# A 3x3 convolution on one core: the first load in two transfers, and rows of one-word loads between the stores

## The chip, the core and the metric

The kernel runs on one core of one Trainium2 chip. The metric is the device time of one execution in microseconds, as the median of several runs. A profile of one execution, taken by the hardware profiler, goes with it; its times count from the span's start, and its own span is a little different from the measured time.

## The reference

Sixteen images of 64 channels and 64 x 64 pixels are convolved with 128 filters of 3 x 3, padding 1, all in float32. Nine tenths of the weights are zero, at random places; the kernel makes no use of that.

```python
x_pad = np.pad(x, ((0, 0), (0, 0), (pad, pad), (pad, pad)), mode='constant')
output = np.zeros((batch, c_out, h, w), dtype=np.float32)
...
                        if weight[co, ci, kh, kw] != 0:
                            output[b, co] += weight[co, ci, kh, kw] * x_pad[b, ci, kh:kh+h, kw:kw+w]
```

The input is 16.8 MB, the output 33.6 MB.

## The kernel before

The 16 images are taken as eight pairs. A pair's 2 x 64 channels lie on the 128 partitions (`xs[p]`, bfloat16), so that one image uses the upper half of TensorE's rows and the other the lower half. Each pair is computed in four blocks of 16 rows.

Loads. All of the input but 32 rows is loaded by GpSimd's DMA queue, which casts float32 to bfloat16 on the way: the lower half of pair 0, pairs 1 to 3 and a part of pair 4 at once (L63 to L77), the rest one pair at a time behind the additions of pairs 1 to 5 (L196 to L199). The weights (`w_sb`, L60) and the first 32 rows of pair 0 (`x_head`, L62, `HEAD = 32`) go through SyncE's queue (SP) in float32. `x_head` is a buffer of the output pool and is cast in three pieces by `cast_x`: rows 0 to 9 by VectorE (L123), rows 9 to 18 and 18 to 32 by ScalarE (L130 and L133). The first eight output rows need only the first piece, the next eight the second too.

Computing. The weights are cast, transposed by TensorE and combined into five groups. Block 0 of pair 0 is computed directly (`direct`, L159). All others go through `twos` (L166): GpSimd adds neighbouring rows into `s`, TensorE makes one shared product from it (copied out of PSUM by ScalarE as `pc`) and one for the even and one for the odd rows, and VectorE adds `pc` to those (L183) into the output tile `o`. Until the input is there, TensorE runs matmuls on zeros (`keep_busy`, L84).

Stores. When the four blocks of a pair are done, SP stores both images, 2 MB each (L209). The last pair is stored in halves of 1 MB (L206): two behind block 1, two behind block 3. Output tiles come from a pool of seven buffers, `x_head` among them, so a tile's first write waits for the store of the tile seven before it.

The order on SP is the order of the code: an instruction that waits holds up all behind it. Every transfer that SP issues takes the next of eight completion semaphores in turn. Where a semaphore is taken again, the program has a wait on it first, until its former transfer has landed. So the wait of each transfer on SP is for the one eight before it (and, for a store, for VectorE's last addition). Behind the stores of pair 1 there are four loads of one word each into `spare`, which nothing reads (L216).

A transfer over 128 partitions has 128 packets of data, eight on each of the core's 16 DMA engines, and one event per engine when it has landed.

Of the kernel before, what the change touches and what calls it, by code (L numbers as in the profile page):

```python
# [8 lines left out]
FP32 = mybir.dt.float32  # L9
# [18 lines left out]
def kernel(  # L28
# [6 lines left out]
    nc = tc.nc  # L35
# [2 lines left out]
    C_OUT, _, KH, KW = weight.shape  # L38
    assert (B, C_IN, H, W) == (16, 64, 64, 64) and (C_OUT, KH, KW) == (128, 3, 3)
    NP = B // 2  # L40
    HEAD = 32

    const_pool = ctx.enter_context(tc.tile_pool(name="const", bufs=1))
    x_pool = ctx.enter_context(tc.tile_pool(name="x", bufs=1))
# [10 lines left out]
    def pair(p):  # L55
        return x[2 * p : 2 * p + 2].rearrange("n i h w -> (n i) h w")
# [2 lines left out]
    w_sb = const_pool.tile([C_OUT, C_IN * KH * KW], FP32, name="w_sb")  # L59
    nc.sync.dma_start(out=w_sb, in_=weight.rearrange("o i kh kw -> o (i kh kw)"))  # L60
    x_head = o_pool.tile([128, H, W], FP32, name="o")
    nc.sync.dma_start(out=x_head[:, 0:HEAD, :], in_=pair(0)[:, 0:HEAD, :])  # L62
    nc.gpsimd.dma_start(out=xs[0][:, HEAD:H, :], in_=pair(0)[:, HEAD:H, :])  # L63
    ident = const_pool.tile([128, 128], BF16, name="ident")
    make_identity(nc, ident)

    def load(p, a=0, b=H):
        nc.gpsimd.dma_start(out=xs[p][:, a:b, :], in_=pair(p)[:, a:b, :])  # L68
# [15 lines left out]
    def keep_busy(n):  # L84
        for _ in range(n):
            nc.tensor.matmul(idle_ps, idle_rhs[:, 0:128], idle_rhs, start=True, stop=True)  # L86
# [13 lines left out]
    def cast_x(copy, a, b):  # L100
        copy(out=xs[0][:, a:b, :], in_=x_head[:, a:b, :])  # L101
# [12 lines left out]
    def difference(g, wps):  # L114
        nc.vector.tensor_tensor(out=wT[:, g], in0=wps, in1=wT[:, G1], op=SUB)  # L115
# [11 lines left out]
    ps2 = transposed(G2)  # L127
    nc.scalar.copy(out=wT[:, G2], in_=ps2)
    keep_busy(7)
    cast_x(nc.scalar.copy, 9, 18)  # L130
    difference(G01, ps0)
    difference(G21, ps2)
    cast_x(nc.scalar.copy, 18, HEAD)  # L133


    def product(terms, rows):
# [22 lines left out]
    def direct(p, o, r0, rows):  # L159
        ps = product(  # L160
            [(xs[p], G1, r0, 1), (xs[p], G0, r0 - 1, 1), (xs[p], G2, r0 + 1, 1)], rows
        )
        nc.scalar.copy(out=o[0][:, r0 : r0 + rows, :], in_=ps[0])  # L163
        nc.vector.tensor_copy(out=o[1][:, r0 : r0 + rows, :], in_=ps[1])  # L164

    def twos(p, o, r0):  # L166
        t0 = r0 // 2
        s = s_pool.tile([128, 8, W], BF16, name="s")
        nc.gpsimd.tensor_tensor(  # L169
            out=s, in0=xs[p][:, r0 : r0 + 16 : 2, :], in1=xs[p][:, r0 + 1 : r0 + 16 : 2, :], op=ADD  # L170
        )
        shared = product([(s, G1, 0, 1)], 8)
        pc = []
        for n in range(2):
            c = p_pool.tile([128, 8, W], FP32, name="pc")
            nc.scalar.copy(out=c, in_=shared[n])  # L176
            pc.append(c)
        even = [(xs[p], G21, r0 + 1, 2), (xs[p], G0, r0 - 1, 2)]
        odd = [(xs[p], G01, r0, 2), (xs[p], G2, r0 + 2, 2)]
        for first, terms in ((r0, even), (r0 + 1, odd)):  # L180
            ps = product(terms, 8)
            for n in range(2):
                nc.vector.tensor_tensor(  # L183
                    out=o[n][:, first : r0 + 16 : 2, :], in0=ps[n], in1=pc[n], op=ADD
                )

    for p in range(NP):
        o = [o_pool.tile([C_OUT, H, W], FP32, name="o") for _ in range(2)]
        last = p == NP - 1
        for blk in range(4):  # L190
            r0 = 16 * blk
            if BLOCKS[p][blk] == "T":
                twos(p, o, r0)


                if p == 1 and blk == 3:  # L196
                    load(EARLY, CUT, H)
                elif blk == 3 and p in LATER:
                    load(*LATER[p])  # L199
            else:  # L200
                for r, rows in ((r0, 8), (r0 + 8, 8)):
                    direct(p, o, r, rows)
            if last and blk % 2 == 1:
                for n in range(2):
                    rows = slice(r0 - 16, r0 + 16)
                    nc.sync.dma_start(out=out[2 * p + n][:, rows, :], in_=o[n][:, rows, :])  # L206
        if not last:
            for n in range(2):
                nc.sync.dma_start(out=out[2 * p + n], in_=o[n])  # L209
        if p == 1:  # L210

            spare = const_pool.tile([1, 4], FP32, name="spare")
            for k in range(4):
                nc.sync.dma_start(out=spare[:, k : k + 1], in_=weight[0:1, 0, 0, 0:1])  # L216


# [28 lines left out]
```

## Time and profile before

| | |
|---|---|
| median of 3 runs | 126.06 us (125.97 to 126.77) |
| span of the profiled execution | 127.2 us |
| PE, VectorE, ScalarE, GpSimd busy | 111.3, 82.4, 38.9, 41.7 us |
| DMA: queue of SP | 34.90 MB, 66.0% of 16 engines' time |
| DMA: queue of GpSimd | 7.86 MB (as written, in bfloat16), 30.0% |
| stores issued (first of each pair) | 26.0, 38.8, 51.6, 64.4, 77.2, 90.0, 102.8 us; halves 109.1 and 115.6 |
| one-word loads issued | 39.9 to 44.6 us |

How to read the lines of the profile: a group has the line, the engine, the operation, what it writes and reads, how often, and times. SPq is SP's sequencer, which issues transfers; the number behind it is how long the issue took, not the transfer. "DMA to landing" counts from the issue until the last of the 16 engines has finished. PEclk is the clock that TensorE was granted, in tenths of the full one. The DMA share is the mean busy share of the 16 engines; packets are counted in the slice in which they start, so it can stand a little above 1.

### The profile page before, as it was taken

To read this page: it belongs to the slowest core of one execution; us is meant where nothing else is said; L and a number is where in the kernel's file an instruction comes from. 1 tells how busy PE (TensorE), PEld (TensorE's weight loads), DVE (VectorE), ACT (ScalarE), POOL (GpSimd) and SP (SyncE) were. 2 spreads that over 40 slices of the span, in tenths; PEclk is the share of its full clock that TensorE was granted. 3 is DMA by queue.
4 is the path that set the end of the run, shared out by engine and by line. 5 is a ranking of instruction groups with operands and counts; after the bars stand their busy time and mean duration, and the time that the engine had idled before them with its cause. 6 is when DMAs were issued, how large, how long until landed. Compare 5 with 4: busy or idle time off the path is not lost.

```text
span 127.2 us, 2468 instructions
## 1 busy us (share of the span) xinstructions
PE 111.3 (87%) x989; PEld 57.9 (46%) x989; DVE 82.4 (65%) x135; ACT 38.9 (31%) x71; POOL 41.7 (33%) x47
## 2 busy tenths in 40 slices
PE   6939999999999999999999999999999999991000
PEld 2414455555555555555555555555555555550000
DVE  0305357787778777877787778777877787775000
ACT  4504343333333333333333333333333333330000
POOL 6405433353335333533353335333333330000000
PEclk9995999999999999999999999999999999999755
DMA  4999999659999999999999999999999999999991
GB/s 131 346 228 214 222 222 206 137 247 412 299 323 397 419 281 299 330 428 330 296 322 430 353 345 420 413 374 345 421 417 412 433 433 438 412 422 415 435 410 77
DMA packets 4339, 42.91 MB, mean 337 GB/s; under 512 B 488, under 2 KB 488, under 8 KB 1256
## 3 DMA queue, kind: packets, MB, share of 16 engines
q1 hardware_dynamic: 2888, 34.90, 66.0%
q0 software_dynamic: 1440, 7.86, 30.0%
q8 instruction: 7, 0.11, 0.3%
q14 instruction: 4, 0.03, 0.1%
HBM read 17.07 MB, written 33.55 MB: 398 GB/s over the span
## 4 chain that ended last, share of the span: by engine, by line
PE 82%; DMA 6%; DVE 1%; issue 1%; DVEq 0%; SPq 0%
PE ps L150 82%; DMA o<-in_x_dram 6%; DVE o L183 1%; DVEq L242 0%; DVE x L101 0%; SPq L60 0%; DVEq L183 0%
## 5 line engine op out<-in xcount | busy, mean ns | idle before, releaser
L150 PE MATMUL ps<-x,wT 64*128 64x504 bf16 (+3 forms) x780 | 90.5, 379 | 2.3 <-DVE x L101 2.3
L183 DVE TENSOR_TENSOR o<-ps,pc 128x512 f32<-128x512 f32 x124 | 77.8, 685 | 22.1 <-PE ps L150 19.8
L150 PEld LDWEIGHTS <-wT 64*128 64x128 bf16 x966 | 55.3, 95 | 52.0 <-issue 4.7
L169 POOL TENSOR_TENSOR s<-x 128x512 bf16<-128x512 bf16 x31 | 35.6, 1151 | 61.2 <-PE ps L150 42.7
L176 ACT COPY pc<-ps 128x512 f32<-128x512 f32 x62 | 33.3, 589 | 64.0 <-issue 61.8
L150 PE MATMUL ps<-s,wT 64*128 64x512 bf16 (+1 forms) x186 | 25.7, 377 | 0.0
L86 PE MATMUL ps<-idle_rhs 128*128 128x512 bf16 x14 | 5.5, 562 | 1.2 <-DVE idle_rhs L81 1.2
L68 POOL DMA_DIRECT2D x<-in_x_dram x9 | 5.0, 560 | 0.0
L164 DVE COPY o<-ps 128x512 f32<-128x512 f32 x2 | 1.4, 692 | 3.7 <-PE ps L150 3.7
L101 DVE CAST x<-o 128x576 bf16<-128x576 f32 x1 | 0.5, 460 | 4.6 <-DMA o<-in_x_dram 4.6
L86 PEld LDWEIGHTS <-idle_rhs 128*128 128x128 bf16 x14 | 1.8, 136 | 3.6 <-issue 2.2
L105 DVE CAST w_bf<-w_sb 128x192 bf16<-128x192 f32 (+1 forms) x4 | 1.1, 357 | 2.4 <-DMA w_sb<-in_weight_dram 2.4
L101 ACT CAST x<-o 128x576 bf16<-128x576 f32 (+1 forms) x2 | 1.5, 802 | 3.5 <-DMA o<-in_x_dram 3.5
L163 ACT COPY o<-ps 128x512 f32<-128x512 f32 x2 | 1.2, 585 | 4.1 <-PE ps L150 4.1
L105 ACT ACT_TABLE_LOAD x1 | 1.3, 1283 | 0.7 <-PEq L231 0.7
L105 ACT CAST w_bf<-w_sb 128x64 bf16<-128x64 f32 (+1 forms) x2 | 0.7, 416 | 1.6 <-DMA w_sb<-in_weight_dram 1.6
L111 PE MATMUL ps<-ident,w_bf 128*128 128x128 bf16 x9 | 1.2, 309 | 0.0
L111 PEld LDWEIGHTS <-w_bf 128*128 128x128 bf16 x9 | 0.8, 130 | 0.8 <-DVE w_bf L105 0.7
L115 DVE TENSOR_TENSOR wT<-ps,wT 128x384 bf16<-128x384 f32 x2 | 1.0, 547 | 0.0
L63 POOL DMA_DIRECT2D x<-in_x_dram x1 | 0.7, 693 | 0.8 <-POOLq L231 0.8
L81 DVE MEMSET idle_rhs<- 128x256 uint32 x1 | 0.3, 272 | 0.9 <-PEq L231 0.9
L124 ACT CAST wT<-ps 128x384 bf16<-128x384 f32 x1 | 0.5, 478 | 0.4 <-PE ps L111 0.4
(8 smaller groups left out, 1.9 us busy)
## 6 DMA issues: line engine op xcount, KB each, us to landing
out_dram<-o SPq DMA_DIRECT2D x14, 2048.0 KB, 15.1
x<-in_x_dram POOLq DMA_DIRECT2D x5, 1024.0 KB, 15.9
out_dram<-o SPq DMA_DIRECT2D x4, 1024.0 KB, 10.8
x<-in_x_dram POOLq DMA_DIRECT2D x3, 512.0 KB, 13.3
o<-in_x_dram SPq DMA_DIRECT2D x1, 1024.0 KB
x<-in_x_dram POOLq DMA_DIRECT2D x1, 640.0 KB, 15.4
x<-in_x_dram POOLq DMA_DIRECT2D x1, 384.0 KB, 21.9
w_sb<-in_weight_dram SPq DMA_DIRECT2D x1, 288.0 KB
```

What stands on the lines that cost most here:

```text
L68: nc.gpsimd.dma_start(out=xs[p][:, a:b, :], in_=pair(p)[:, a:b, :])
L86: nc.tensor.matmul(idle_ps, idle_rhs[:, 0:128], idle_rhs, start=True, stop=True)
L101: copy(out=xs[0][:, a:b, :], in_=x_head[:, a:b, :])
L105: copy(out=w_bf4[:, g, a:b, :], in_=w_v[:, k : k + b - a, :])
L111: nc.tensor.matmul(wps[:, j, :], src, ident, start=True, stop=True)
L115: nc.vector.tensor_tensor(out=wT[:, g], in0=wps, in1=wT[:, G1], op=SUB)
L150: nc.tensor.matmul(ps[n][:, lo:hi, c_lo:c_hi], tap(g, kw, n), src[q, a:b:step, c_lo + kw - 1 : c_hi + kw - 1], start=(i == 0), stop=(i == ...
L163: nc.scalar.copy(out=o[0][:, r0 : r0 + rows, :], in_=ps[0])
L164: nc.vector.tensor_copy(out=o[1][:, r0 : r0 + rows, :], in_=ps[1])
L169: nc.gpsimd.tensor_tensor(out=s, in0=xs[p][:, r0 : r0 + 16 : 2, :], in1=xs[p][:, r0 + 1 : r0 + 16 : 2, :], op=ADD)
L176: nc.scalar.copy(out=c, in_=shared[n])
L183: nc.vector.tensor_tensor(out=o[n][:, first : r0 + 16 : 2, :], in0=ps[n], in1=pc[n], op=ADD)
```

## The change

The load of the first 32 rows becomes two transfers, of rows 0 to 18 and 18 to 32; the bound 18 of the casts is now called `FIRST`, and the casts are the same. The four one-word loads behind pair 1 become three. Behind the stores of pair 3 there are now 16 small loads: the n-th reads one word into each of n partitions, n from 1 to 16. The same 16 stand behind the first two half stores of the last pair, ahead of its last two. All go through SP, into columns of `spare` that nothing reads. No other instruction is added, left out or moved.

```diff
-    HEAD = 32
+    FIRST, HEAD = 18, 32
...
-    nc.sync.dma_start(out=x_head[:, 0:HEAD, :], in_=pair(0)[:, 0:HEAD, :])
+    for a, b in ((0, FIRST), (FIRST, HEAD)):
+        nc.sync.dma_start(out=x_head[:, a:b, :], in_=pair(0)[:, a:b, :])
...
-    cast_x(nc.scalar.copy, 9, 18)
+    cast_x(nc.scalar.copy, 9, FIRST)
...
-    cast_x(nc.scalar.copy, 18, HEAD)
+    cast_x(nc.scalar.copy, FIRST, HEAD)
...
+    spare = const_pool.tile([16, 40], FP32, name="spare")
+
+    def one_word(at, n):
+        nc.sync.dma_start(out=spare[0:n, at : at + 1], in_=weight[0:n, 0, 0, 0:1])
+
...
+            if last and blk == 1:
+                for n in range(1, 17):
+                    one_word(18 + n, n)
...
-            spare = const_pool.tile([1, 4], FP32, name="spare")
-            for k in range(4):
-                nc.sync.dma_start(out=spare[:, k : k + 1], in_=weight[0:1, 0, 0, 0:1])
+            one_word(0, 1)
+            one_word(1, 1)
+            one_word(2, 1)
+        if p == 3:
+            for n in range(1, 17):
+                one_word(2 + n, n)
```

## The prediction

> **What bounds the kernel now.** I read the page's slices first, then windows by stage, then the stores' landings, and last what SP waited for. From the page:
>
> ```profile
> span 127.2 us, 2468 instructions
> ...
> PEclk9995999999999999999999999999999999999755
> DMA  4999999659999999999999999999999999999991
> ...
> HBM read 17.07 MB, written 33.55 MB: 398 GB/s over the span
> ```
>
> The DMA digits are 9 from end to end but for the start, the end and one hole in slices 7 and 8. The windows give the hole and the tail (columns: stretch, busy time of the engines, granted clock, DMA share, GB/s):
>
> ```profile
> 24.00:28.00 4.00, 4.00 (x42) 2.21 (x40) 3.37 (x6) 1.07 (x2) 1.67 (x2) 1.00 0.45 156
> 28.00:64.00 36.00, 36.00 (x340) 19.10 (x338) 28.26 (x46) 11.81 (x22) 13.68 (x13) 1.00 1.02 347
> 116.00:124.00 8.00, 0.00 (x0) 0.00 (x0) 0.16 (x1) 0.00 (x0) 0.00 (x0) 0.70 1.00 422
> ```
>
> PE and DVE stop by 116 and the DMA engines run on at a share of 1.00: from 28 us on the kernel lasts as long as its transfers. The chain of waits names PE for 82%, but it follows the last instruction and stops at 116; the 10 us behind it are the backlog of stores. The only idle DMA time in the middle is the hole, 4 us at 0.45, so 2.2 us: the early loads are done and the first store goes out at 26.0. So the price list is simple: what idles the 16 engines after 28 us is added to the span one for one; what fills the hole is gained, up to 2.2 us.
>
> The landings (answers for the output tensor by window; the first pair of stores, the fourth, and the first halves of the last):
>
> ```profile
> DMA to landing us min/median/max: 6.7/11.2/15.7
> L209 SPq DMA_DIRECT2D out_dram<-o x2: 332/800/1268, 64.4 to 65.0; - x2
> DMA to landing us min/median/max: 15.0/17.6/20.2
> L206 SPq DMA_DIRECT2D out_dram<-o x2: 332/650/969, 109.1 to 109.7; - x2
> DMA to landing us min/median/max: 9.8/10.8/11.7
> ```
>
> A 2 MB store into empty queues lands after 6.7 us. Pair 3's second store, issued at 65.0, lands at 65.0+20.2 = 85.2: SP's transfers land 15 to 20 us after issue. The last pair's halves of block 1 land at 118.9 and 121.4; pair 6's second store landed at 116.5, so a store's worth of data takes 4.9 us. The last half landed at 126.3, and 0.9 us of closing follow. And SP:
>
> ```profile
> SPq L209 <- DVE o L183: 90.8, 14, 24.3
> ```
>
> So far SP waits for VectorE alone: no transfer waited for an older one.
>
> **Part 1, the head in 18 and 14 rows.** PE's start hangs on the head:
>
> ```profile
> 9.33 0.46 DVE L101 CAST x<-o 128x576 bf16<-128x576 f32 x1 [4.61 <-DMA o<-in_x_dram]
> 9.84 5.67 PE L150 MATMUL ps<-x,wT 64*128 64x512 bf16 x36 [2.34 <-DVE x L101]
> ```
>
> By the head's 16 landing events, 15 engines finish by 6.6 us and one at 9.30: that one alternates its eight 8 KB packets (0.32 us) with eight GpSimd load packets (0.32). At 18 rows its packets are 0.32×18/32 = 0.18, so eight of them end 8×0.14 = 1.1 us sooner: the first cast at 8.2, PE at 8.7. The second 14 rows land near 9.3 as now, their cast takes 0.7, and block 1 needs them only after the 36 direct matmuls: free. The extra issue on SP (0.4) is followed by 24 us of waiting: free. PE's granted clock is 0.50 from 9.9 to 13.3, behind an idle time of 2.3 us; 1.1 us less idle may spare that half speed, about 1.7 us more. So pair 0's stores go out 1.1 to 2.8 us earlier. The hole takes 1.1 to 2.2 of it; I take 1.5, and all later transfers land that much earlier.
>
> The Trainium skill, "TensorE: Matmul & The Clock Gate", section "What's actually happening", says that the gate judges free-running windows of about 3.4 us; the half-speed stretch of 3.4 us agrees with it. By that rule the drop hangs on where the window falls, and an idle time of 1.2 us may still be followed by it.
>
> **Part 2, four one-word loads become three behind pair 1.** SP's next store is ready at 51.6, the loads end at 44.6: free, with 7 us to spare.
>
> **Part 3, 16 loads behind pair 3's stores and 16 behind the last pair's first two halves.** The words themselves are nothing (4-byte packets of SP's queue took 9 ns in the median). The waits are not. In the changed program's order on SP every transfer takes the next of eight semaphores in turn, and waits until the transfer eight before it has landed. In the program of before this is so too, but the stores are far enough apart that it never bound. Sixteen words in a row go round the eight twice. Behind pair 3, words 1 to 6 wait for transfers that land by 72.5; word 7 waits for pair 3's first store (79.4) and word 8 for its second (85.2, now 85.2−1.5 = 83.7). Words 9 to 16 wait for words 1 to 8, which are in by then. Queued behind word 8 on SP: nine word issues with its own, then pair 4's stores, which VectorE has had ready since about 76. At 83.7 SP's queues on the DMA engines are empty, and GpSimd's last load has some 2 us of work left: this is idle DMA time. Nobody else waits for it: the last pair's second output tile reuses the buffer of pair 4's first store (seven buffers), but that lands at 97 to 101 and is wanted after 101.
>
> The unknown is the pitch of word issues. Two rows bound it:
>
> ```profile
> 0.74 0.38 SPq L60 DMA_DIRECT2D w_sb<-in_weight_dram  x1
> 1.18 0.42 SPq L62 DMA_DIRECT2D o<-in_x_dram  x1
> ...
> 39.92 1.15 SPq L216 DMA_DIRECT2D spare<-in_weight_dram  x1
> 41.12 0.98 SPq L216 DMA_DIRECT2D spare<-in_weight_dram  x1
> 42.15 1.07 SPq L216 DMA_DIRECT2D spare<-in_weight_dram  x1
> 43.26 1.30 SPq L216 DMA_DIRECT2D spare<-in_weight_dram  x1
> ```
>
> 0.44 us with empty DMA queues, (44.57−39.92)/4 = 1.16 with full ones. Stores show the same: the second of a pair took 0.34 at 26.5 and 0.5 to 1.4 later. The words that count go out when the queues have run dry, so I lean to the empty row: 0.7 for the first batch (a load still runs), 0.5 for the second.
>
> The sum, in span time. Pair 4's first store goes out at 83.7+9×0.7 = 90.0. Six stores and two halves follow without a gap: 6.7 for the first from empty, 6×4.9 for the rest, so the last of them lands at 90.0+36.1 = 126.1. Again word 7 waits for the first of these halves, word 8 for the second: the last two halves, ready at 114, go out at 126.1+9×0.5 = 130.6, land 6.7 later (2 MB from empty), and 0.9 closes: 138.2. In general 127.3+9×(sum of both pitches). The median of 126.06 is 1.1 below the profiled span of 127.2; I take that off: 137.1.
>
> The Trainium skill, "DMA: Bandwidth & Descriptors", section "Rules for kernel authors", speaks against the loads: transfers under 64 KB are mostly overhead; its section "Anatomy of one DMA — SWDGE (gpsimd) path" gives, for GpSimd's path, about 2.0 us fixed a transfer. If the 18 loads each paid that in turn, an estimate by that page would be 127.3+18×2.0−1.1 = 162 us; the row of 1.16 us a word says that they don't wait for one another's landing.
>
> **Rivals.**
> (a) The forecast, pitches summing to 0.88 to 1.6: 127.3+7.9−1.1 = 134.1 to 140.6; with the whole hole filled 133.4.
> (b) The pitch belongs to the one-word form, not to the load: four of four took 0.98 or more, while two second stores under load took 0.5. Then 2×1.16: 127.3+20.9−1.1 = 147.1, and 147.5 with only 1.1 gained at the head; 148.5 at 1.24, between the words' mean and the longest (1.30).
> (c) Faster: the eight-deep wait is met when SP comes to it, and the words cost nothing. It decides at two points: word 16 out before about 76, and again before 114. Then only the head counts: 126.06−1.1 = 125.0, at best 123.9. For it: no such wait has yet bound a transfer in this trace. Against it: pair 3's second store lands at 85.2, and word 8 cannot pass that.
> (d) Only the second batch costs, the first finding a cover: then 9×0.5 plus the drained queue, landing of the halves near 120 and 120+4.5+6.7+0.9−1.1 = 131. Against it: between 84 and 90 nothing else is queued.
>
> **How the numbers follow.** (a) 0.62, (b) 0.30, (d) 0.04, (c) 0.03, 0.01 for no visible change. The likeliest gives 137; the range, with both pitches, 133.4 to 148.5, leaves out (c), (d) and some 0.05 of the rest. About 1% (1.3 us) is what this kernel's measurement can tell; slower by more than that: 0.96, faster 0.03, same 0.01.
>
> **What would show it.** DMA slices near zero around 86 to 90 us and again near 127 to 131; pair 4's first store issued near 90, not 77; SP waiting for DMA landings of the output, which it now never does before the end; first cast near 8.2 us. Wrong if pair 4's stores still go out at 77, if word issues differ from 0.44 to 1.16, or if VectorE stalls on an output buffer.

## The result and the profile after

The changed kernel takes 139.06 us (137.77 to 141.76, six runs) against 126.11 us for the kernel before, run beside it: a ratio of 1.099, 95% interval 1.095 to 1.103. It is 13 us slower, where 11 were forecast (137.1 against 126.06); the predicted 137.1 is 2.0 us too low.

The page of the changed kernel, the lines that answer to those of before:

```profile
span 137.7 us, 2500 instructions
...
PEclk9999999999999999999999999999999997555555
DMA  4999999999999999999999994099999999991193
...
HBM read 17.07 MB, written 33.55 MB: 368 GB/s over the span
```

The bytes are the same. The hole in slices 7 and 8 (counted from 0) is gone, and two new ones are there: slices 24 and 25 (82.6 to 89.5 us) and slices 36 and 37 (123.9 to 130.8 us). The windows size them (stretch, busy time of the engines, granted clock, DMA share, GB/s):

```profile
64.00:82.00 18.00, 18.00 (x172) 9.54 (x168) 14.38 (x23) 5.37 (x10) 6.93 (x8) 1.00 1.01 377
82.00:84.00 2.00, 2.00 (x22) 1.02 (x18) 1.27 (x3) 1.07 (x2) 1.15 (x1) 1.00 0.92 201
84.00:90.00 6.00, 6.00 (x60) 3.25 (x58) 4.69 (x9) 2.15 (x4) 2.31 (x2) 1.00 0.17 54
90.00:124.00 34.00, 23.42 (x220) 12.18 (x216) 19.84 (x32) 7.52 (x14) 4.63 (x4) 0.88 1.00 421
124.00:131.00 7.00, 0.00 (x0) 0.00 (x0) 0.00 (x0) 0.00 (x0) 0.00 (x0) 0.50 0.14 52
```

From 84 to 90 the DMA engines have 17% of their work, from 124 to 131 14%: 6×0.83 + 7×0.86 = 11.0 us idle. In the first hole PE is busy throughout: computing goes on and its output waits. SP's waits say for what:

```profile
SPq L218 <- DVE o L184: 67.3, 13, 22.5
SPq L191 <- DMA out_dram<-o: 23.1, 7, 5.6
```

L191 is the one-word load. In the kernel before, the transfers that SP issued waited for VectorE alone; now seven of the words wait 23.1 us in all for stores to land. SP in order of time:

```profile
62.98 1.95 SPq L218 DMA_DIRECT2D out_dram<-o  x2
64.98 23.77 SPq L191 DMA_DIRECT2D spare<-in_weight_dram  x16
88.85 14.16 SPq L218 DMA_DIRECT2D out_dram<-o  x6
107.75 1.64 SPq L212 DMA_DIRECT2D out_dram<-o  x2
109.44 20.18 SPq L191 DMA_DIRECT2D spare<-in_weight_dram  x16
129.72 0.84 SPq L212 DMA_DIRECT2D out_dram<-o  x2
```

Sixteen words hold SP for 23.8 and 20.2 us. Pair 4's first store goes out at 88.85, where it went at 77.2; the last halves go out at 129.72, where they went at 115.6. The eighth words go out at 84.06 and 126.22, just when pair 3's second store (84.05) and the second half of block 1 (126.20) have landed on the last of the 16 engines.

Some executions of a kernel are longer as a whole; the medians here count them, the ratios leave them out, and the profiled execution of before was such a one, its span 127.2 us where the same kernel mostly had 124.1 to 125.0 beside the experiments. The times there were 1.7 to 2.6 us above the spans.

### The profile page after: what moved, and what is told of

It is laid out like the page before. It is cut to its first block, busy times and chain, and to the rows that moved or that the text cites. A ratio compares the mean times of both kernels' runs of the same rounds, so it can differ in the third digit from the quotient of the medians.

```text
span 137.7 us, 2500 instructions
## 1 busy us (share of the span) xinstructions
PE 109.7 (80%) x989; PEld 56.9 (41%) x989; DVE 82.5 (60%) x135; ACT 38.9 (28%) x71; POOL 41.7 (30%) x47
## 4 chain that ended last, share of the span: by engine, by line
PE 71%; DMA 7%; DVE 1%; POOL 1%; ACT 1%; issue 1%; SPq 1%; DVEq 0%
PE ps L151 71%; DMA o<-in_x_dram 7%; DVE o L184 1%; POOL s L170 1%; ACT x L102 1%; DVEq L251 0%; SPq L63 0%; SPq L60 0%; DVEq L184 0%
## 5 line engine op out<-in xcount | busy, mean ns | idle before, releaser
L151 PE MATMUL ps<-x,wT 64*128 64x504 bf16 (+3 forms) x780 | 88.8, 373 | 0.0
L151 PEld LDWEIGHTS <-wT 64*128 64x128 bf16 x966 | 54.4, 94 | 51.5 <-issue 3.2
```

Of the source, the lines that this page charges most:

```text
L151: nc.tensor.matmul(ps[n][:, lo:hi, c_lo:c_hi], tap(g, kw, n), src[q, a:b:step, c_lo + kw - 1 : c_hi + kw - 1], start=(i == 0), stop=(i == ...
```

## The experiments

"Head" is the load of pair 0's first 32 rows, a "row of words" the 16 small loads at one place. Where a ratio is given it is to the kernel before, run beside it, with the 95% interval. The kernels below have three words behind pair 1 but for the one that has none.

**The head alone.** The changed kernel without its two rows of words:

```diff
-            if last and blk == 1:
-                for n in range(1, 17):
-                    one_word(18 + n, n)
...
-        if p == 3:
-            for n in range(1, 17):
-                one_word(2 + n, n)
```

> The changed kernel without its two rows of 16 words (head in two transfers and three words behind pair 1 stay). Theory of the waits (SP's eight-deep semaphore turn makes the words wait for the newest stores, so the stores behind them go out onto empty queues): all of the loss is gone and the head's gain is left, 1.4 us by the first store (24.6 in place of 26.0): ratio 0.988 to 0.993, about 124.9 us. Rival (the split head costs: its second part lands at 11.7 us and PE waits 2.5 us for it): ratio 1.00 or above.

Measured: 128.53 us, ratio 1.012 (1.004 to 1.020). The loss of 13 us is gone with the words, all but 2 us of it, and the gain of the head isn't there: the split makes the kernel slower by about 1%. The rival is right on this part.

**The row behind pair 3 alone**, and **the row between the last halves alone**, each with the head in one transfer as before:

```diff
-    for a, b in ((0, FIRST), (FIRST, HEAD)):
-        nc.sync.dma_start(out=x_head[:, a:b, :], in_=pair(0)[:, a:b, :])
+    nc.sync.dma_start(out=x_head[:, 0:HEAD, :], in_=pair(0)[:, 0:HEAD, :])
```

> Head in one transfer, 16 words behind pair 3 only. Theory of the waits: word 8 goes out when pair 3's second store lands (85.2), nine issues take some 4.8 us as in the changed kernel (84.06 to 88.85), so pair 4's first store goes out at 90 and lands near 96.4 where it landed at 92.1 before: 4.3 us more, ratio 1.034, with the last halves not held up. Rival (a price for each word wherever it stands: 13 us over 32 words, 0.4 us each): 16 x 0.4 = 6.5 us, ratio 1.05.

> Head in one transfer, 16 words between the last pair's halves only. Theory of the waits: word 8 at 121.4 (landing of the second half of block 1), nine issues 3.5 us, last halves out at 124.9, landed 7.1 later at 132.0, span 132.9 for 127.2: 5.7 us more, ratio 1.045. The costs of this and of the row behind pair 3 add up, with the head's gain taken off, to the whole change. Rival (0.4 us a word): ratio 1.05, equal to that of the row behind pair 3.

Measured: 131.64 us, ratio 1.043 (1.036 to 1.050), for the first; 131.60 us, ratio 1.040 (1.036 to 1.044), for the second: 5.2 us each. Each time the theory's path is in the trace. Behind pair 3, word 8 goes out at 83.25 and pair 4's first store at 86.74; between the halves, word 8 at 118.37 and the next half at 121.87. But the first was to be 1.034, which lies outside its interval, while the rival's 1.05 lies at its edge; 16 words cost nearly the same in both places, as the rival had it. So these two runs alone don't part the theories. The next do.

**Rows of six words**, once with the split head and once with the head in one transfer:

```diff
-                for n in range(1, 17):
+                for n in range(1, 7):
```

> The changed kernel with rows of 6 words (1 to 6 partitions) in place of 16, at both places. Theory of the waits: two stores and six words are eight, so the store behind the words waits for the store just ahead of them, while the next older data is still queued; no idle time of the DMA engines: as fast as the head alone, within 0.4 us. Rival (0.4 us a word): 12 words cost 4.9 us, ratio 1.03.

> Head in one transfer, rows of 6 words at both places, three words behind pair 1. Theory of the waits: the first store behind each row waits for the first transfer ahead of the row, the second for the second, so data is always queued: ratio 0.997 to 1.004. Rival (a price for each word): 12 words at 0.3 to 0.4 us, ratio 1.03 to 1.04.

Measured: with the split head 128.95 us, ratio 1.012 (1.006 to 1.017), no more than the head alone; with the head in one transfer 126.66 us, ratio 1.002 (1.000 to 1.004). Twelve words cost 0.3 us. In the second, SP does wait for landings, and it costs nothing:

```profile
SPq L217 <- DVE o L183: 68.1, 12, 20.5
SPq L217 <- DMA out_dram<-o: 11.9, 2, 6.0
```

```profile
82.00:92.00 10.00, 10.00 (x96) 4.59 (x94) 7.97 (x14) 3.22 (x6) 3.46 (x3) 1.00 1.02 410
```

Two stores wait 11.9 us in all for older ones, but from 82 to 92 the DMA share stays at 1.02: when the first of them goes out (76.64), pair 3's second store is still under way. It is not the wait that costs, but having nothing queued while it lasts.

**Rows of seven words**, one word more at each place:

```diff
-                for n in range(1, 17):
+                for n in range(1, 8):
```

> The same with rows of 7 words. Theory of the waits: now the first store behind each row waits for the transfer just ahead of the row, so it goes out onto empty queues, but without the issues of words 8 to 16: the cost measured for 16 words (5.2 us at each place) less the 3.5 us between word 8 and the store: 1.7 us a place, 3.5 us in all, ratio 1.028. Rival (a price for each word): two words more than with six, 0.6 to 0.8 us more, ratio 1.005 above that run.

Measured: 130.56 us, ratio 1.033 (1.028 to 1.038). The seventh word at each place costs 3.9 us for the two, where the first six cost 0.3 for all twelve. Of pair 4's stores one waits for an older store now, and in the same window the DMA share is lower:

```profile
SPq L217 <- DMA out_dram<-o: 6.1, 1, 6.1
```

```profile
82.00:92.00 10.00, 10.00 (x98) 5.34 (x96) 7.97 (x13) 3.22 (x6) 3.47 (x3) 1.00 0.85 349
```

The DMA share falls from 1.02 to 0.85: now the first store behind the row waits for pair 3's second store, the newest one (landed at 83.51), and goes out at 83.57 onto queues that SP has left empty. A price for each word cannot make this step; a turn of eight semaphores puts it between six and seven.

**No words at all**, the kernel before without its four:

```diff
-            spare = const_pool.tile([1, 4], FP32, name="spare")
-            for k in range(4):
-                nc.sync.dma_start(out=spare[:, k : k + 1], in_=weight[0:1, 0, 0, 0:1])
```

> The kernel of before without its four one-word loads. Theory of the waits: they stood in time in which SP waited anyway, so nothing changes: ratio 0.997 to 1.003. Rival (the words do something for the transfers behind them, by shifting them on the engines): over 1% either way.

Measured: 126.77 us, ratio 1.004 (1.000 to 1.007). That is a hair above the theory's 1.003 and far from the rival's 1%. The four words behind pair 1 do next to nothing; whether there is a third of a per cent in them, this can't tell.

**The split head with GpSimd's loads later.** No rows of words:

```diff
-    nc.gpsimd.dma_start(out=xs[0][:, HEAD:H, :], in_=pair(0)[:, HEAD:H, :])
     ident = const_pool.tile([128, 128], BF16, name="ident")
+    for _ in range(5):
+        nc.gpsimd.memset(ident, 0.0)
     make_identity(nc, ident)
+    nc.gpsimd.dma_start(out=xs[0][:, HEAD:H, :], in_=pair(0)[:, HEAD:H, :])
```

> Head in two transfers, three words behind pair 1, no rows of words; GpSimd makes the identity matrix, with five more memsets of it, ahead of its first load, so that all its loads are issued some 1.5 us later. Theory (the second part of the head loses its place: its packets alternate one for one with those of GpSimd's first load, land at 11.7 us or later, and PE waits for the cast and the addition): with that load later the second part lands by 7.5, no wait of PE behind block 0, and the time is that of before: ratio 0.99 to 1.003. Rival (the split head itself is slow, for instance by its smaller packets): ratio stays at 1.012.

Measured: 126.97 us, ratio 1.004 (1.000 to 1.007), where the same without the delay had 1.012 (1.004 to 1.020). These intervals overlap, so the times alone only point to the theory; the traces show the step itself. First the changed kernel (start, duration, engine, work; in brackets the idle time ahead of it and what ended it), ScalarE and PE:

```profile
6.16 0.67 ACT L102 CAST x<-o 128x576 bf16<-128x576 f32 x1
11.73 0.94 ACT L102 CAST x<-o 128x896 bf16<-128x896 f32 x1 [4.90 <-DMA o<-in_x_dram]
```

```profile
7.45 3.98 PE L151 MATMUL ps<-x,wT 64*128 64x512 bf16 x36
13.95 0.82 PE L151 MATMUL ps<-s,wT 64*128 64x512 bf16 x6 [2.52 <-POOL s L170]
```

The first part comes early, the second at 11.7; its cast and GpSimd's addition come behind it, and PE stands still for 2.52 us. Now with GpSimd's first load issued at 2.74 in place of 1.24:

```profile
7.50 0.94 ACT L104 CAST x<-o 128x896 bf16<-128x896 f32 x1 [0.91 <-DMA o<-in_x_dram]
```

```profile
7.80 3.98 PE L153 MATMUL ps<-x,wT 64*128 64x512 bf16 x36
11.62 0.81 PE L153 MATMUL ps<-s,wT 64*128 64x512 bf16 x6
```

The second part is there at 7.5, and PE runs through. So the second part is late because it shares the engines with GpSimd's load. In the changed kernel the second part's 128 packets start between 5.3 and 10.6 us (median 7.6), GpSimd's first 128 between 4.8 and 9.1 (median 6.8). That fits a packet of 0.15 us getting its turn after one of 0.32: eight such turns make 3.8 us, and the first of the 16 engines was done at 9.2. That some engines took until 11.7 this doesn't explain.

Compare the kernel without words, whose head is one transfer:

```profile
6.83 1.51 ACT L101 CAST x<-o 128x576 bf16<-128x576 f32 x2 [0.95 <-DMA o<-in_x_dram]
```

The whole head is there at 6.8 and PE starts at 7.34. This, not the 9.3 of the profile of before, is what the split had to beat.

**Both rows with the head in one transfer**, and the same with **one partition for every word**:

```diff
-                    one_word(18 + n, n)
+                    one_word(18 + n, 1)
...
-                one_word(2 + n, n)
+                one_word(2 + n, 1)
```

> The changed kernel with the head in one transfer: both rows of 16 words. Theory (the rows cost by their waits, at two places that don't share time; the split head costs the rest): the two single rows add up, 5.2+5.2 us: ratio 1.083; the changed kernel at 1.099 is above it by the split head's 1.2 to 1.6%. Rival (the split head's loss is hidden once the rows hold up the stores): ratio 1.099 as for the changed kernel.

> The same, but each of the 32 words goes into one partition alone. In the changed kernel's trace words issued onto empty queues took 0.27 us for 7 partitions and 0.38 for 16. Theory (an issue costs some 0.01 us for each partition, on top of a fixed part): nine issues in 2.8 us where words of 8 to 16 partitions took 3.5: 0.7 us less at each place, ratio 1.071. Rival (the form with fewer than 16 partitions is no cheaper, or the first word alone is): ratio 1.083.

Measured: 138.12 us, ratio 1.092 (1.089 to 1.096), and 135.83 us, ratio 1.072 (1.065 to 1.080). The first is between the theory's 1.083 and the rival's 1.099, and its interval holds neither: the rows cost 11.8 us together and 5.2 each alone. For the second, SP from word 8 of the first row, each run's own line:

```profile
84.19 3.40 SPq L190 DMA_DIRECT2D spare<-in_weight_dram  x9
```

```profile
83.33 2.59 SPq L190 DMA_DIRECT2D spare<-in_weight_dram  x9
```

Nine issues take 3.40 us with words over 8 to 16 partitions and 2.59 over one: 0.8 us a row, near the expected 0.7. The two rows' issues are 1.6 of the 2.3 us between the two kernels. In the profiled executions another 0.9 stands before them, since word 8 is released at 83.33 and not at 84.19. So it is luck that 1.072 meets the 1.071, which was reckoned from 1.083 for both rows.

## Why the prediction was right, and where not

**The mechanism held.** The words wait for the transfer eight before them, word 8 for the newest store; the stores behind go out onto empty queues; what idles the engines after 28 us is added to the span. The step between six and seven words shows the first, the windows the second, and for the third there are 11.0 us of idle time against 13 us of loss, about 1 of which goes with the split (139.06 against 138.12 us). The Trainium skill ("DMA: Bandwidth & Descriptors", section "Why a DMA increments its semaphore by 16 and not by 1") asks for one semaphore per transfer in flight; a program that keeps to it with eight has eight in flight at most, and the runs show what it costs when the transfer waited for is the newest large one. Of the marks named beforehand, the two holes, the issue of pair 4's first store (near 90 forecast, 88.85 measured) and SP's waits for landings came; the first cast came at 6.16, not near 8.2. Of the signs of being wrong, VectorE's stall on an output buffer didn't come, but one did: issues outside 0.44 to 1.16 us. Behind word 8 they took 0.29 to 0.39, and one 1.58.

**The terms, span against span:** word 8 at 83.7, measured 84.06. Nine issues 6.3, measured 4.79. From pair 4's first issue to the last landing ahead of the second wait 36.1, measured 37.35. Nine issues 4.5, measured 3.50. Landing of the last halves 6.7, measured 7.08. Closing 0.9 as it was. In all 138.2 against 137.7: misses of both signs that nearly cancel, and that is luck. So is the first term: 83.7 is 85.2, from the profile with the span of 127.2 us, less a gain of 1.5 that didn't come; in the kernel without words pair 3's second store lands at 83.03. (The prediction's short form, 127.3 plus the issues, should have 127.4 by its own terms.)

**The pitch** was leaned the right way, and not far enough: 0.53 us a word in the first row, where the second issue took 1.58, and 0.39 in the second. The load that was to slow the first row was nearly through: from 84.06 on, GpSimd's packets were 0.2 us of work for the 16 engines, not 2. With the first row alone (83.25 to 86.74) the pitch was 0.39 there too. What made the one issue long isn't known. Rival (b), that the form of the transfer sets it, falls: in the same trace words issued one behind the other took 1.0 to 1.3 us while stores were under way, and 0.29 to 0.39 onto empty queues. The Trainium skill's rule on small transfers ("DMA: Bandwidth & Descriptors", section "Rules for kernel authors"), beside which the prediction had set an estimate of 162 us, doesn't give the price here: the words of the second row from the eighth on each landed 1.3 to 1.6 us after their issue, several at a time, and what stood on the path was the issue of a word, not its overhead as a transfer.

**The step that failed is part 1.** "The second 14 rows land near 9.3 as now ... free" is wrong: they landed at 11.7 and cost PE 2.52 us. I had counted the packets of GpSimd's load against the first part only. The gain of 1.1 to 2.2 us was also reckoned from an execution whose head came late on one engine (9.30, the others by 6.6) and which had a hole for it; in the kernel without words the window from 24 to 28 has a DMA share of 1.06, and an earlier store has no idle time to fill. Measured alone, the split costs 1.2%. With both rows in the kernel it is 139.06 against 138.12, 0.7% more, with intervals that overlap. The half-speed stretch of the clock is absent from the changed kernel's page, but from that of the kernel without words too, so it was no gain of the split either. Nor does idle time alone decide on it here: PE's 2.52 us in the changed kernel weren't followed by half speed, the 2.34 of before were.

**The conversion failed too.** I took 1.1 us off the span, because the median of before stood 1.1 below the profiled span. In the changed kernel's profiled execution the time, 139.49, is 1.8 above its span of 137.7. That makes the forecast 2.9 us too low; the sum of the span, 0.5 too long, and the median, 0.4 below the profiled execution's time, leave 2.0.

**Rival (d), one row without cost**, falls with the two single rows; **(c), faster**, with the result.

**Open:** why two rows together cost 1.3 us more than their sum, an excess of 0.9% that is hardly larger than its uncertainty. By the last landings in the profiled executions, against the kernel without words, it is 1.4 us, and 0.9 of that is there before the first row's eighth word goes out: word 8 behind pair 3 waits for that pair's second store, which landed at 84.17 with both rows and at 83.23 with the first alone, in kernels that are the same up to there. In both, 15 of the 16 engines had it by 82.2, and one came later. Why it was later in one than in the other, a single execution of each can't tell.

## What to carry to other kernels

Count the transfers on a queue between two that matter: where completion semaphores are taken in turn, a small transfer that nobody reads can make the next large one wait for the newest store, and the price is the idle time of the DMA engines, not the words. Here two stores and six words, eight in all and the turn's length, were nearly free; a seventh word was not. And before a gain is reckoned from one profiled execution, set its span against several others: here the hole that the split was to fill was in that one, and in none of the profiles of the seven kernels of the experiments that have the head in one transfer (DMA share 1.04 to 1.08 from 24 to 28 us).

## What the hardware showed that I had not expected

Words issued one behind the other onto empty queues cost little, and by the number of partitions: 0.25 us for one (nine at a pitch of 0.29), 0.29 for 9, 0.39 for 16, against 1.0 to 1.3 while stores were under way. It is the second of two issues that is dear then, not the first: a word that had waited took 0.27 us (at 78.27) with pair 3's second store still under way. A word doesn't overtake what is queued ahead of it: the first word behind pair 3, issued at 64.98, landed at 81.93. And a transfer cut in two didn't keep its place beside another queue: the 32 rows as one transfer were cast from 6.83 on, as two the last 14 came at 11.7.
